# Seven products in the first feed-forward stage, moved modulation sections, and the mixers' two-operand work on VectorE

## The chip, the core and the metric

The kernel runs on one core of a Trainium2 chip. The metric is device time in microseconds (us). TensorE (PE) multiplies and PEld loads its weights, VectorE (DVE), ScalarE (ACT) and GpSimd (POOL) do the elementwise work, SyncE (SP) issues the transfers. A 32-bit value is multiplied as a high and a low part (both in the matmul's 32-bit format), and one product takes three matmuls: high by high, high by low, low by high.

## The reference

640 tokens (128 of a prompt, 512 of a grid) of width 1024 go through two layers. Each layer has three sublayers: a feed-forward network of width 2816, a mixer of three head groups, and a second feed-forward network. A modulation made from the condition scales, shifts and gates each of them.

```python
def swiglu(u, lp, j):
    return (jax.nn.silu(u @ lp['ffn_w_gate'][j]) * (u @ lp['ffn_w_up'][j])) @ lp['ffn_w_down'][j]
...
def trunk_layer(x, cond, lp, ropes, ctx):
    mod = (jax.nn.silu(cond) @ lp['w_mod'] + lp['b_mod'])[:, None, :]
    sh1, sc1, g1, sh2, sc2, g2, sh3, sc3, g3 = jnp.split(mod, N_MOD, axis=-1)
    x = layer_norm(DEEPNORM_ALPHA * x + 0.5 * g1 * swiglu(x * (1 + sc1) + sh1, lp, 0), lp['ln_g'][0], lp['ln_b'][0])
    y, ctx_out = mixer(x * (1 + sc2) + sh2, lp, ropes, ctx)
    x = layer_norm(DEEPNORM_ALPHA * x + g2 * y, lp['ln_g'][1], lp['ln_b'][1])
    x = layer_norm(DEEPNORM_ALPHA * x + 0.5 * g3 * swiglu(x * (1 + sc3) + sh3, lp, 1), lp['ln_g'][2], lp['ln_b'][2])
    return x, ctx_out
```

The mixer projects its input to 1696 columns, runs a recurrent scan, a grouped attention and a latent attention side by side, and projects back.

## The kernel before

**Stages.** The program is a list of steps in six stages: f00, m0, f01 (layer 0) and f10, m1, f11 (layer 1). f is a feed-forward network, m a mixer. The program text sets the order of TensorE's instructions. VectorE and ScalarE run in an order that a scheduler fixes at build time, in which `high_priority(offset=...)` moves an instruction ahead. All engines take their instructions in that fixed order. The weights come as 512 KB tiles through SP's queue into shared buffers (`raw`), in the order of the steps.

**A feed-forward stage.** The 2816 hidden columns are 22 m-tiles of 128. For each tile a gate and an up weight tile are split into a high part (L194, ScalarE) and a low part (L199, VectorE). In the classic form (`mtile`, L526 to L528) gate and up take 96 matmuls of 128x320 each tile. In the form with seven products (`ffn_fast`, L1083) the gate and up matrices of a tile are blocks of a 2x2 product that needs seven block products in place of eight, 84 matmuls; sums of the weight blocks (L1051), their splits (L1055 on ScalarE, L1059 on VectorE) and sums of the input are made for it, and the products are gathered by L1113 to L1137. f01, f10 and f11 use it from tile 3 on (`CLASSIC = 3`). f00 has a function of its own, `ffn_steps`, with the classic form for all 22 tiles. After every three tiles a down product (L821 to L823 in f00, L1195 to L1197 in the others) multiplies the hidden tiles with the down weights. f00 scales each down result by the gate (L828, VectorE) and adds it to the residual (L830, POOL). The others add the plain result to a sum (L1208, VectorE), having put x in DRAM, and scale and blend at the end.

**The opening of f00.** Modulation sections of layer 0 are needed before anything else. Tiles 0 and 1 are multiplied without the shift, which is added as a late bias (L674 and L679), and tile 2 follows (`start2`).

**Sections.** A section (layer, index) is one 1024-wide ninth of the modulation: eight 512 KB weight tiles, multiplied with two conditions. On TensorE it is eight steps, each of which the trace shows as 8 matmuls (L364). On VectorE it is 32 instructions of 128x512 (L329, L331), and 16 short matmuls (L340) sum over the partitions at the end. `PLAN` says in which stage a section stands. Those in a mixer's list and the one in `start2` run on TensorE, those in the third list of a feed-forward stage on VectorE. In `ffn_fast` they are fed by `trickle`, one instruction for every `MGAP` turns of the step list.

**A mixer.** Projections of 128 columns (`proj`, split by L194 and L199), the scans (L1386 to L1467), the norms and rotary products (L1523 to L1545), the attention (L1888 scores, L1902 and L1903 row maxima, L1904 exponentials, L1913 scaling on POOL, L1922 and L1850), and the output projection, whose result is scaled (L2279) and added to the residual (L2282). `ONV` names the two-operand instructions that `eng` puts on VectorE; the others are POOL's.

Of the kernel before, what the change touches and what calls it, by code (L numbers as in the profile page):

```python
# [18 lines left out]
P = 128  # L19
# [37 lines left out]
ONV = ('ladd', 'lix', 'mqg', 'swk0')  # L57
# [26 lines left out]
MGAP = 12  # L84
# [25 lines left out]
class Kern:  # L110
# [456 lines left out]
    def ffn_steps(self, l, j, mods):  # L567

        nc, I = self.nc, self.I
        env = {}  # L570
        S = []

        def B(dt=F32):
            return env["pool"].tile([P, TOK], dt, tag="B", bufs=11, name=self.nm("b"))

        def DW(shape):
            return env["pool"].tile(shape, F32R, tag="DW", bufs=8, name=self.nm("dw"))

        def T(shape):
            return env["pool"].tile(shape, F32, tag="T", bufs=3, name=self.nm("t"))  # L580

        def G4(shape):
            return env["pool"].tile(shape, F32, tag="G", bufs=4, name=self.nm("g"))

        jj = (0, 2)[j]
        hs = {}
        halves = {}
        dws = []
        for m in range(NM):
            g, u, d = {}, {}, {}  # L590
            fs = slice(m * P, (m + 1) * P)
            halves[m] = (g, u, d)

            def w_in_view(w):
                return w[l, j][:, fs].rearrange("(k p) f -> p k f", p=P)
# [3 lines left out]
            dl, dsp = self.weight(I["ffn_w_down"][l, j][fs, :], [P, D], d, DW)  # L599

            def silu(g, cut=HALF):
                for a, b in self.chunks(g["s"], g["ps"], cut):
                    nc.scalar.activation(a, b, AF.Silu)

            def hout(m, g, u, cut=HALF):
                s = g["s"]
                for a, b in self.chunks(s, u["ps"], cut):
                    nc.vector.tensor_mul(a, a, b)
                hh, hl = B(F32R), B(F32R)
# [4 lines left out]
            dws.append((dl, dsp))  # L614
            late_g, late_d = ((), ()) if m == 0 else LATE[l == 0 and j == 0].get(m, ((), (m,)))

            def gbody(m=m, g=g, late=[fn for i in late_g for fn in dws[i][1]]):
                g["ps"] = self.p2("pg")
                g["s"] = B()
                late = list(late)  # L620
                for c in range(2):
                    for _ in self.mtile(g["ps"], g, c):
                        yield
                        for _ in range(min(2, len(late))):
                            late.pop(0)()
                for fn in late:
                    fn()
                silu(g)


            def ubody(m=m, g=g, u=u, late=[fn for i in late_d for fn in dws[i][1]]):
                u["ps"] = self.p2("pu")
                if l == 0 and j == 0 and m == 4:
                    for i in range(DEPTH):
                        self.setup_vec(i)
                late = list(late)
                for c in range(2):
                    for _ in self.mtile(u["ps"], u, c):
                        yield
                        if late:  # L640
                            late.pop(0)()
                for fn in late:
                    fn()
                hout(m, g, u)

            def first(m=m, g=g, u=u):
                env["cm"] = self.tc.tile_pool(name=f"ffn{l}{j}", bufs=1, reuse_waits="tile")
                env["pool"] = env["cm"].__enter__()
                self.B_DW = DW
                g["ps"], u["ps"] = self.p2("pu"), self.p2()  # L650
                g["s"] = B()
                yield from self.mtile(g["ps"], g, 0, CUT)
                self.after_a()
                yield from self.mtile(u["ps"], u, 0, CUT)
                yield from self.mtile(g["ps"], g, 1, CUT)
                silu(g, CUT)
                yield from self.mtile(u["ps"], u, 1, CUT)
                hout(m, g, u, CUT)

            def biased(m, g, u):  # L660
# [29 lines left out]
                hh, hl = B(F32R), B(F32R)  # L690
                nc.scalar.copy(hh, s)
                nc.vector.tensor_sub(hl, s, f(hh))
                hs[m] = (hh, hl)
# [7 lines left out]
            def start(gsp, usp, g1=g, u1=u):  # L701


                g0, u0, _ = halves[0]
# [24 lines left out]
                env["cm"] = self.tc.tile_pool(name=f"ffn{l}{j}", bufs=1, reuse_waits="tile")  # L729
# [23 lines left out]
            def start2(m=m, g=g, u=u):  # L753

                g["ps"], u["ps"] = self.p2(), self.p2()
                g["s"] = B()
                todo = deque(self.next_steps)
                for h, k0 in ((g, 0), (u, 0), (g, 4), (u, 4)):
                    if k0 and self.late_bias:
                        self.bg.append(self.late_bias.pop(0)())  # L760
                    for k in range(k0, k0 + 4):
                        self.block(h, k)
                        yield CAP2 if h is u and k >= 6 else 0
                        if not todo:
                            continue
                        st = todo.popleft()
                        while not st.ready():
                            self.feed()
                        for _ in st.body():
                            yield  # L770
                silu(g)
                hout(m, g, u)
                if OEND == 2:
                    self.order.__exit__(None, None, None)
            if l == 0 and j == 0 and m == 0:
                self.first_w = gl, gsp, ul, usp
                S.append(None)
            elif l == 0 and j == 0 and m == 1:
                ul, usp = self.weight(w_in_view(I["ffn_w_up"]), [P, KT, P], u, lambda s: self.X(s, F32R))
                S[0] = Step([lambda i=i: self.shift_load(i) for i in range(4, 8)], [], lambda a=gsp, b=usp, go=start: go(a, b))  # L780
                self.second_w = gl, ul
                S.append(Step())
                S.append(Step())
            elif l == 0 and j == 0 and m == 2:
# [4 lines left out]
                lds = [gl, ul] + [st.loads[0] for st in self.next_steps] + [dws[i][0] for i in late_d]  # L789
                S.append(Step(lds, gsp + usp, start2, 0))  # L790
                S.append(Step([], [fn for i in late_d for fn in dws[i][1]]))
            elif m == 0:
                S.append(Step([gl, ul], gsp + usp, first))
            elif l == 0 and j == 0 and m == 3:
                S[-2].loads.insert(G3, gl)
                S.append(Step([dws[i][0] for i in late_g], gsp, gbody))
                S.append(Step([ul] + [dws[i][0] for i in late_d], usp, ubody))
            else:
                S.append(Step([gl] + [dws[i][0] for i in late_g], gsp, gbody))
                S.append(Step([ul] + [dws[i][0] for i in late_d], usp, ubody))  # L800
            S.extend(mods.get(m, []))


        def down(ci, ms):
            def body():
                lastc = ci == len(CHUNKS) - 1
                if ci == 0:
                    env["gate"] = self.gate_tiles(l, jj, G4, True)
                if lastc:
                    self.ln_begin(l, jj)  # L810
                for t in range(NT):
                    gt = env["gate"][1 if t == 0 else 0]
                    x = self.x[t]
                    for h in range(2):
                        pt = self.p1()
                        for i, m in enumerate(ms):
                            hh, hl = hs[m]
                            d = halves[m][2]
                            hsl = slice(h * 512, (h + 1) * 512)
                            ts = slice(t * P, (t + 1) * P)  # L820
                            nc.tensor.matmul(pt, lhsT=hh[:, ts], rhs=d["hi"][:, hsl], start=(i == 0), stop=False)  # L821
                            nc.tensor.matmul(pt, lhsT=hh[:, ts], rhs=d["lo"][:, hsl], start=False, stop=False)
                            nc.tensor.matmul(  # L823
                                pt, lhsT=hl[:, ts], rhs=d["hi"][:, hsl], start=False, stop=(i == len(ms) - 1)
                            )
# [5 lines left out]
                        if lastc:  # L831
                            self.ln_part(t, h, 2)
# [1761 lines left out]
```

## Time and profile before

| | before |
|---|---|
| median of 3 runs | 2546.53 us (2545.23 to 2547.19) |
| profiled execution | 2543.89 us, span 2541.8 us |
| PE busy | 2443.6 us (96%) |
| DVE, ACT, POOL busy | 74%, 42%, 16% |

The profiled execution has 2.1 us outside its span. TensorE's matmul records overlap, since each is shown from its start to a modelled end; what a matmul costs in a row of them is the distance from one start to the next.

### The profile page before, as it was taken

To read this page: it belongs to the slowest core of one execution; us is meant where nothing else is said; L and a number is where in the kernel's file an instruction comes from. 1 tells how busy PE (TensorE), PEld (TensorE's weight loads), DVE (VectorE), ACT (ScalarE), POOL (GpSimd) and SP (SyncE) were. 2 spreads that over 40 slices of the span, in tenths; PEclk is the share of its full clock that TensorE was granted. 3 is DMA by queue.
4 is the path that set the end of the run, shared out by engine and by line. 5 is a ranking of instruction groups with operands and counts; after the bars stand their busy time and mean duration, and the time that the engine had idled before them with its cause. 6 is when DMAs were issued, how large, how long until landed. Compare 5 with 4: busy or idle time off the path is not lost. (4 is left out here: it accounts for less than half of the span.)

```text
span 2541.8 us, 39941 instructions
## 1 busy us (share of the span) xinstructions
PE 2443.6 (96%) x15804; PEld 2218.4 (87%) x15804; DVE 1891.1 (74%) x3161; ACT 1068.9 (42%) x1882; POOL 411.2 (16%) x389
## 2 busy tenths in 40 slices
PE   8899999999999999999999999999999999999997
PEld 7789898988867999999889999988987799999986
DVE  5887778687754797777789777778785578777777
ACT  3212111246674444343354434435657534433432
POOL 2320221113632100000200000020373210000022
PEclk9999999999999999999999999999999999999999
DMA  8655445522233233333333333332232323333321
GB/s 286 197 152 155 141 147 185 158 69 80 95 90 113 67 132 111 98 100 100 108 91 124 113 96 100 100 108 82 91 112 90 97 76 100 110 107 104 113 92 50
DMA packets 271394, 288.53 MB, mean 114 GB/s; under 512 B 13436, under 2 KB 223976, under 8 KB 271208
## 3 DMA queue, kind: packets, MB, share of 16 engines
q1 hardware_dynamic: 271208, 285.99, 36.3%
q8 instruction: 124, 2.03, 0.3%
q14 instruction: 62, 0.51, 0.1%
HBM read 268.17 MB, written 16.21 MB: 112 GB/s over the span
## 5 line engine op out<-in xcount | busy, mean ns | idle before, releaser
L1083 PE MATMUL pb<-u,w 128*128 128x320 f32 x2736 | 420.4, 309 | 1.7 <-DVE b L1129 1.7
L1083 PEld LDWEIGHTS pb<-u,w 128*128 128x128 f32 x2736 | 406.7, 188 | 4.0 <-issue 2.4
L526 PE MATMUL p<-u,w 128*128 128x320 f32 (+2 forms) x1104 | 348.3, 316 | 8.6 <-ACT u L517 6.4
L527 PE MATMUL p<-u,w 128*128 128x320 f32 (+2 forms) x1104 | 345.8, 314 | 1.8 <-DVE u L518 1.8
L528 PE MATMUL p<-u,w 128*128 128x320 f32 (+2 forms) x1104 | 344.4, 313 | 0.0
L1083 PE MATMUL pb<-s,w 128*128 128x320 f32 x2052 | 322.0, 309 | 1.3 <-ACT b L1136 1.3
L1083 PEld LDWEIGHTS pb<-s,w 128*128 128x128 f32 x2052 | 306.0, 188 | 3.7 <-ACT b L1136 1.9
L1055 ACT CAST w<-raw 128x512 fp32r<-128x512 f32 x399 | 239.8, 619 | 162.8 <-DVE raw L1051 107.5
L1059 DVE TENSOR_TENSOR w<-raw,w 128x512 fp32r<-128x512 f32 x399 | 272.6, 696 | 34.9 <-ACT w L1055 34.2
L194 ACT CAST dw<-raw 128x1024 fp32r<-128x1024 f32 x87 | 89.1, 1051 | 452.6 <-PE p L1196 263.9
L331 DVE SCALAR_TENSOR_TENSOR x<-raw,cst,x 128x512 f32<-128x512 f32 x308 | 236.9, 815 | 33.3 <-DMA raw<-in_w_mod 33.2
L1195 PE MATMUL p<-dw,b 128*128 128x512 f32 x630 | 249.7, 396 | 11.3 <-DVE x L1208 10.1
L1196 PE MATMUL p<-dw,b 128*128 128x512 f32 x630 | 245.8, 390 | 0.0
L1197 PE MATMUL p<-dw,b 128*128 128x512 f32 x630 | 245.5, 390 | 0.0
L526 PEld LDWEIGHTS p<-u,w 128*128 128x128 f32 x1104 | 211.5, 192 | 13.7 <-ACT u L517 7.4
L527 PEld LDWEIGHTS p<-u,w 128*128 128x128 f32 x1104 | 211.7, 192 | 2.9 <-DVE u L518 2.5
L528 PEld LDWEIGHTS p<-u,w 128*128 128x128 f32 x1104 | 211.1, 192 | 0.3 <-DVE w L199 0.3
L194 ACT CAST w<-raw 128x1024 fp32r<-128x1024 f32 x100 | 104.8, 1050 | 241.3 <-PE p L527 162.3
L1208 DVE TENSOR_TENSOR x<-x,p 128x512 f32<-128x512 f32 x150 | 102.8, 685 | 110.5 <-PE p L1197 110.5
L1195 PEld LDWEIGHTS p<-dw,b 128*128 128x128 f32 x630 | 118.2, 188 | 47.3 <-DVE x L1208 21.6
L199 DVE TENSOR_TENSOR w<-raw,w 128x1024 fp32r<-128x1024 f32 x100 | 124.1, 1242 | 44.6 <-ACT w L194 40.5
L1157 POOL TENSOR_SCALAR x<-x 128x1024 f32<-128x1024 f32 x6 | 6.3, 1056 | 871.1 <-PE p L1197 438.3
(367 smaller groups left out, 4815.7 us busy)
## 6 DMA issues: line engine op xcount, KB each, us to landing
raw<-in_w_mod SPq DMA_DIRECT2D x132, 512.0 KB
raw<-in_ffn_w_gate SPq DMA_DIRECT2D x88, 512.0 KB
raw<-in_ffn_w_up SPq DMA_DIRECT2D x88, 512.0 KB
raw<-in_ffn_w_down SPq DMA_DIRECT2D x88, 512.0 KB
raw<-in_w_in SPq DMA_DIRECT2D x26, 512.0 KB
xd<-x SPq DMA_DIRECT2D x25, 512.0 KB
raw<-in_w_out SPq DMA_DIRECT2D x16, 512.0 KB
t<-xd SPq DMA_DIRECT2D x30, 256.0 KB
```

The lines of the kernel that those rows point to most:

```text
L194: nc.scalar.copy(h, hold["raw"])
L199: nc.vector.tensor_sub(l, hold["raw"], f(hold["hi"]))
L331: e.scalar_tensor_tensor(acc[:, cs], hold["raw"][:, cs], c, acc[:, cs], op0=ALU.mult, op1=ALU.add)
L526: nc.tensor.matmul(out, lhsT=wh, rhs=xh, start=start, stop=False)
L527: nc.tensor.matmul(out, lhsT=wh, rhs=xl, start=False, stop=False)
L528: nc.tensor.matmul(out, lhsT=wl, rhs=xh, start=False, stop=stop)
L1055: nc.scalar.copy(w[:, 0], at(src))
L1059: nc.vector.tensor_sub(w[:, 1], at(src), f(w[:, 0]))
L1083: nc.tensor.matmul(out, lhsT=a1, rhs=b1, start=(start and k == 0 and i == 0), stop=(k == 3 and i == 2), skip_group_check=not start,)
L1195: nc.tensor.matmul(pt, lhsT=hh[:, ts], rhs=d["hi"][:, cs], start=(i == 0), stop=False)
L1196: nc.tensor.matmul(pt, lhsT=hh[:, ts], rhs=d["lo"][:, cs], start=False, stop=False)
L1197: nc.tensor.matmul(pt, lhsT=hl[:, ts], rhs=d["hi"][:, cs], start=False, stop=(i == len(ms) - 1))
```

## The change

`ffn_steps` goes. Layer 0's first feed-forward stage is made by `ffn_fast` too: `opening` has tiles 0 to 2 (the late bias for 0 and 1, tile 2 in `third`), tile 3 is classic, and tiles 4 to 21 take seven products. The stage therefore writes x to DRAM and blends at its end as the others do; the first down product has tiles 0 to 2. Section (0,2) leaves TensorE for VectorE. VectorE's sections go from 8, 1, 1, 1 in f00, f01, f10, f11 to 3, 2, 2, 1; TensorE's from one in f00 and two in each mixer to five in m0 and three in m1. The gap of `trickle` follows the number of sections in the stage: 11 turns for one, 5 for two, 3 for three. In the mixers the splits of the projection weights are issued with priority, and seven two-operand instructions (named in `ONV`, the rotary product of the latent query, the addition to the residual) move from POOL to VectorE.

```diff
-ONV = ('ladd', 'lix', 'mqg', 'swk0')
+ONV = ('ladd', 'lix', 'lir', 'lmul', 'mqg', 'mkg', 'swk0', 'swk1', 'swq0', 'swq1')
...
-    "f00": [[], [], [(0, 3), (0, 4), (0, 5), (0, 6), (0, 7), (1, 0), (1, 1), (1, 2)]],
-    "m0": [[], [(0, 8), (1, 3)]],
-    "f01": [[], [], [(1, 4)]],
-    "f10": [[], [], [(1, 5)]],
-    "m1": [[], [(1, 6), (1, 7)]],
+    "f00": [[], [], [(0, 2), (0, 3), (0, 4)]],
+    "m0": [[], [(0, 5), (0, 6), (0, 7), (0, 8), (1, 0)]],
+    "f01": [[], [], [(1, 1), (1, 2)]],
+    "f10": [[], [], [(1, 3), (1, 4)]],
+    "m1": [[], [(1, 5), (1, 6), (1, 7)]],
...
-MGAP = 12
+MGAP = 12, 11, 5, 3
...
+                parts(m, g["s"], lambda: self.X([P, TOK], F32R))
+                self.order.__exit__(None, None, None)
+                self.x_d = [self.dp.tile([P, D], F32, name=self.nm("xd")) for _ in range(NT)]
+                for t in range(NT):
+                    nc.sync.dma_start(out=self.x_d[t], in_=self.x[t])
...
+        opens = l == 0 and j == 0
+        classic = CLASSIC + opens
...
+        if opens:
+            S += self.opening(env, hs, B, DW)
+            gate, up = plain(3)
+            for m in range(3):
+                dl, dsp = down_w(m)
+                gate.loads.append(dl)
+                S.append(Step([], dsp))
+            S[-3:] = [gate] + S[-3:] + [down([0, 1, 2], begin=True), up]
...
+        gap = MGAP[sum(len(v) for v in mods.values()) // KT]
...
-                        for _ in range(MGAP):
+                        for _ in range(gap):
...
-                nc.gpsimd.tensor_mul(
+                nc.vector.tensor_mul(
...
+        def urgent(fns):
+
+
+            def wrap(fn):
+                def go():
+                    with self.tc.high_priority(offset=AHEAD):
+                        fn()
...
+            sp = urgent(sp)
...
-                        e = nc.vector if last else nc.gpsimd
-                        e.tensor_add(x[:, cs], x[:, cs], tt)
+                        nc.vector.tensor_add(x[:, cs], x[:, cs], tt)
...
-            plan = spread(PLAN[f"f{l}0"], *((4,) if l == 0 else (4, 16)))
-            new = self.ffn_steps(l, 0, plan) if l == 0 else self.ffn_fast(l, 0, plan)
+            plan = spread(PLAN[f"f{l}0"], *((5, 17) if l == 0 else (4, 16)))
+            new = self.ffn_fast(l, 0, plan)
```

The order of three places shows what moved. First, TensorE in the opening of f00, the end of tile 2's first half (L526 to L528 the tile's matmuls, L364 a step of section (0,2), L666 the late bias). Before:

```order
L526 MATMUL p_80_714<-u_130,dw_680 128x320
L527 MATMUL p_80_714<-u_132,dw_680 128x320
L528 MATMUL p_80_714<-u_130,dw_686 128x320
L364 MATMUL p_82_722<-raw_729,cst 32x256 x4
L526 MATMUL p_79_713<-u_131,dw_640 128x320
L527 MATMUL p_79_713<-u_133,dw_640 128x320
L528 MATMUL p_79_713<-u_131,dw_652 128x320
```

Of the change:

```order
L526 MATMUL p_80_714<-u_130,dw_680 128x320
L527 MATMUL p_80_714<-u_132,dw_680 128x320
L528 MATMUL p_80_714<-u_130,dw_686 128x320
L526 MATMUL p_79_713<-u_131,dw_640 128x320
L527 MATMUL p_79_713<-u_133,dw_640 128x320
L528 MATMUL p_79_713<-u_131,dw_652 128x320
```

The last of the section's eight steps stood there; none of them is left in this tile.

Second, VectorE in f00. Before, at a down product (L828 scales it) and the tile that follows (L608 multiplies gate and up, L611 and L199 split, L331 and L329 are section instructions):

```order
L331 SCALAR_TENSOR_TENSOR x_2621<-raw_2619,cst,x_2621 128x512 x2
L828 TENSOR_TENSOR t_2414<-p_306_2401,g_1054 128x512
L828 TENSOR_TENSOR t_2430<-p_308_2417,g_1057 128x512
L828 TENSOR_TENSOR t_2446<-p_310_2433,g_1054 128x512
L828 TENSOR_TENSOR t_2462<-p_312_2449,g_1057 128x512
L828 TENSOR_TENSOR t_2478<-p_314_2465,g_1054 128x512
L828 TENSOR_TENSOR t_2494<-p_316_2481,g_1057 128x512
L828 TENSOR_TENSOR t_2510<-p_318_2497,g_1054 128x512
L199 TENSOR_TENSOR dw_2562<-raw_2253,dw_2544 128x1024
L199 TENSOR_TENSOR dw_2721<-raw_2342,dw_2703 128x1024
L828 TENSOR_TENSOR t_2526<-p_320_2513,g_1057 128x512
L608 TENSOR_TENSOR b_2313<-b_2313,p_322_2529 128x640
```

Of the change, at a tile of seven products in the same stage (L898 differences of weight blocks, L906 their splits, L960 to L984 gather the products, L760 splits the hidden tile, L331 as before):

```order
L331 SCALAR_TENSOR_TENSOR x_2026<-raw_1917,cst,x_2026 128x512
L331 SCALAR_TENSOR_TENSOR x_2025<-raw_2070,cst,x_2025 128x512 x2
L960 TENSOR_TENSOR pb_1241<-pb_1241,b_2047 128x320
L331 SCALAR_TENSOR_TENSOR x_2026<-raw_2070,cst,x_2026 128x512
L962 TENSOR_TENSOR pb_1239<-pb_1239,b_2047 128x320
L976 TENSOR_TENSOR b_1882<-pb_1240,b_1882 128x320
L906 TENSOR_TENSOR w_2119<-raw_2093,w_2119 128x512
L331 SCALAR_TENSOR_TENSOR x_2026<-raw_2070,cst,x_2026 128x512
L898 TENSOR_TENSOR raw_2093<-raw_2109,raw_2093 128x512
L331 SCALAR_TENSOR_TENSOR x_2025<-raw_2082,cst,x_2025 128x512 x2
L979 TENSOR_TENSOR b_2132<-b_2132,pb_1238 128x320
L906 TENSOR_TENSOR w_2142<-raw_2093,w_2142 128x512
```

Section instructions now stand between the instructions on which the next product waits.

Third, VectorE in the first mixer, among the scans (before: L1440 and L1455, of the change L1303, L1304 and L1318; L199 is the low half of a projection's weight split, L1304 the product that was POOL's L1441). Before:

```order
L1440 SCALAR_TENSOR_TENSOR b_5471<-b_5625,b_5471 128x644
L1440 SCALAR_TENSOR_TENSOR b_5517<-b_5641,b_5517 128x644
L1440 SCALAR_TENSOR_TENSOR b_5563<-b_5658,b_5563 128x644
L1455 SCALAR_TENSOR_TENSOR b_5821<-b_5625,b_5493 128x128
L1455 SCALAR_TENSOR_TENSOR b_5821<-b_5625,vec_108,b_5493 128x512
L199 TENSOR_TENSOR w_5799<-raw_4993,w_5774 128x1024
```

Of the change:

```order
L1318 SCALAR_TENSOR_TENSOR b_5654<-b_5455,vec_108,b_5298 128x512
L1303 SCALAR_TENSOR_TENSOR b_5322<-b_5476,b_5322 128x644
L1304 TENSOR_TENSOR b_5344<-b_5344,b_5322 128x644
L199 TENSOR_TENSOR w_5650<-raw_4464,w_5625 128x1024
L1303 SCALAR_TENSOR_TENSOR b_5368<-b_5492,b_5368 128x644
L199 TENSOR_TENSOR w_5688<-raw_4483,w_5670 128x1024
```

The splits stand before the third scan step of four instead of behind the second scan, and L1304 is new on VectorE.

## Rows read from the trace of the kernel before

**Rows 1.** The page, busy time: us, share of the span, instructions.

```profile
PE 2443.6 (96%) x15804; PEld 2218.4 (87%) x15804; DVE 1891.1 (74%) x3161; ACT 1068.9 (42%) x1882; POOL 411.2 (16%) x389
```

**Rows 2.** Windows: stretch, length, busy us by engine, granted clock, DMA share, GB/s.

```profile
0.00:545.00 545.00, 519.09 (x3411) 468.38 (x3411) 405.75 (x586) 138.28 (x187) 105.30 (x91) 0.99 0.54 168
545.00:875.00 330.00, 313.44 (x2349) 275.90 (x2350) 220.67 (x436) 192.91 (x353) 116.41 (x117) 0.97 0.29 92
875.00:1320.00 445.00, 436.94 (x2596) 403.97 (x2595) 347.92 (x572) 187.14 (x343) 19.74 (x17) 1.00 0.34 102
...
16.00:96.00 80.00, 74.27 (x697) 66.20 (x690) 54.04 (x78) 33.61 (x51) 21.71 (x17) 0.96 0.86 281
...
916.00:1280.00 364.00, 360.12 (x2150) 334.20 (x2150) 276.96 (x448) 148.28 (x274) 16.27 (x12) 1.00 0.37 111
...
655.00:805.00 150.00, 142.88 (x1067) 107.49 (x1066) 89.40 (x216) 105.41 (x205) 57.45 (x66) 1.00 0.33 105
```

**Rows 3.** TensorE's waits, whole span: total us, times, longest.

```profile
PE p L821 <- DVE t L828: 10.3, 15, 1.3
PE p L527 <- DVE w L199: 10.2, 6, 3.0
PE p L1195 <- DVE x L1208: 10.1, 27, 0.8
...
PE p L679 <- DVE b L674: 4.5, 1, 4.5
```

**Rows 4.** Timeline of TensorE: start, length, instruction; f00, then f01.

```profile
122.67 0.31 PE L526 MATMUL p<-u,w 128*128 128x320 f32 x1
122.81 0.31 PE L527 MATMUL p<-u,w 128*128 128x320 f32 x1
...
954.82 2.95 PE L1083 MATMUL pb<-s,w 128*128 128x320 f32 x19
```

**Rows 5.** Timeline of TensorE in f00: section matmuls between a tile's own.

```profile
58.40 0.64 PE L364 MATMUL p<-raw,cst 128*32 128x256 f32 x8
...
60.04 0.64 PE L364 MATMUL p<-raw,cst 128*32 128x256 f32 x8
...
157.90 0.31 PE L528 MATMUL p<-u,w 128*128 128x320 f32 x1
158.14 1.07 PE L340 MATMUL p<-x,sel 128*32 128x256 f32 x16
...
159.39 0.31 PE L527 MATMUL p<-u,w 128*128 128x320 f32 x1
```

**Rows 6.** Timeline of all engines in the opening, with idle before and releaser.

```profile
84.88 1.28 DVE L329 TENSOR_SCALAR x<-raw,cst 128x512 f32<-128x512 f32 x3 [4.90 <-DMA raw<-in_w_mod]
...
86.53 0.37 PE L679 MATMUL p<-ident,b 4*128 4x4 f32 x2 [4.45 <-DVE b L674]
```

**Rows 7.** VectorE's groups, 96 to 545 us, then 916 to 1280 us.

```profile
L331 DVE SCALAR_TENSOR_TENSOR x<-raw,cst,x 128x512 f32<-128x512 f32 x221 | 173.8, 842 | 25.4 <-DMA raw<-in_w_mod 25.4
...
L331 DVE SCALAR_TENSOR_TENSOR x<-raw,cst,x 128x512 f32<-128x512 f32 x28 | 20.3, 747 | 3.1 <-DMA raw<-in_w_mod 3.1
```

**Rows 8.** Windows of VectorE alone, products of f01 and f10.

```profile
960.00:980.00 20.00, 19.88 (x36) 1.00 0.34 100
...
1400.00:1420.00 20.00, 19.82 (x34) 1.00 0.52 153
```

**Rows 9.** Timeline of the first mixer, VectorE, then TensorE.

```profile
620.72 1.19 DVE L199 TENSOR_TENSOR w<-raw,w 128x1024 fp32r<-128x1024 f32 x1
...
621.96 0.39 PE L527 MATMUL p<-w,u 128*128 128x256 f32 x1 [2.96 <-DVE w L199]
```

**Rows 10.** Timeline of TensorE in the first mixer's attention.

```profile
671.48 2.35 PE L364 MATMUL p<-raw,cst 128*32 128x256 f32 x34 [0.58 <-ACT u L1761]
```

**Rows 11.** Groups of POOL and VectorE, whole span.

```profile
L2282 POOL TENSOR_TENSOR x<-x,b 128x256 f32<-128x256 f32 x20 | 18.3, 916 | 54.4 <-DVE b L2279 50.2 <-DMA raw<-in_ffn_w_down 4.1
...
L2282 DVE TENSOR_TENSOR x<-x,b 128x256 f32<-128x256 f32 x20 | 8.4, 422 | 0.4
```

More of the change, by code (lines that the diff above doesn't have):

```diff
@@ L564, in chunks, with opening, parts @@
         return [(s[:, 0:cut], pt[:, 0, 0:cut]), (s[:, cut:TOK], pt[:, 1, 0 : TOK - cut])]
-    def ffn_steps(self, l, j, mods):
+    def opening(self, env, hs, B, DW):
         nc, I = self.nc, self.I
-        env = {}
         S = []
[L573 to L586, printed above, removed]
         halves = {}
-        dws = []
-        for m in range(NM):
-            g, u, d = {}, {}, {}
+        for m in range(3):
+            g, u = {}, {}
             fs = slice(m * P, (m + 1) * P)
-            halves[m] = (g, u, d)
+            halves[m] = (g, u)
             def w_in_view(w):
-                return w[l, j][:, fs].rearrange("(k p) f -> p k f", p=P)
+                return w[0, 0][:, fs].rearrange("(k p) f -> p k f", p=P)
             gl, gsp = self.weight(w_in_view(I["ffn_w_gate"]), [P, KT, P], g, self.W)
             ul, usp = self.weight(w_in_view(I["ffn_w_up"]), [P, KT, P], u, self.W)
[L599 to L609, printed above, removed]
+            def parts(m, s, alloc):
+                hh, hl = alloc(), alloc()
                 nc.scalar.copy(hh, s)
@@ L612, in hout @@
                 hs[m] = (hh, hl)
[L614 to L658, printed above, removed]
             def biased(m, g, u):
@@ L689, in biased @@
                     )
[L690 to L693, printed above, removed]
+                parts(m, s, lambda: B(F32R))
             def kept(g, u):
@@ L788, in ffn_steps @@
                     fn.ready = lambda h=h: "DW" in env and "raw" in h
[L789 to L825, printed above, removed]
-                        tt = T([P, 512])
-                        with self.tc.high_priority(offset=AHEAD):
-                            nc.vector.tensor_mul(tt, pt, gt[h])
-                        e = nc.vector if lastc and (FA or h or t == NT - 1 or self.next_mod) else nc.gpsimd
-                        e.tensor_add(x[:, hsl], x[:, hsl], tt)
-                        if lastc:
-                            self.ln_part(t, h, 2)
-                        yield
-                    if lastc:
-                        self.end_tile(t)
-                if lastc:
-                    env["cm"].__exit__(None, None, None)
-            return Step([], [], body)
@@ L869, in ffn_steps @@
-        out.append(down(*pend))
-        return out
+                S.append(Step([gl, ul], gsp + usp, third, 0))
+        return S
     def ffn_fast(self, l, j, mods):
@@ L952, in gate @@
             def gate():
+                if opens:
+                    env["sums"] = sums()
+                    self.bg.append(env["sums"])
                 g["ps"] = self.p2()
@@ L1174, in body @@
                 if begin:
-                    for _ in self.res:
+                    for _ in () if opens else self.res:
                         pass
@@ L1229, in ffn_fast @@
             S += st + mods.get(m, [])
-        dl, dsp = down_w(CLASSIC - 1)
+        dl, dsp = down_w(classic - 1)
         S[-1].loads.append(dl)
@@ L1262, in rest, with vecs @@
             yield
-        seq = [("A", CLASSIC), ("A", CLASSIC + 1), ("D", 2)]
-        for m in range(CLASSIC, NM):
+        def vecs():
+            for i in range(DEPTH):
+                self.setup_vec(i)
+            yield
+        seq = [("A", classic), ("A", classic + 1)] + ([] if opens else [("D", 2)])
+        for m in range(classic, NM):
             seq.append(("B", m))
@@ L1275, in ffn_fast @@
                 S += part_a(m)
+                if opens and m == classic:
+                    S.append(Step([], [], vecs))
             elif what == "B":
@@ L2030, in mixer_steps @@
         S = []
+        def urgent(fns):
[3 more added lines that the diff above has]
+                        fn()
+                go.ready = fn.ready
+                return go
+            return [wrap(fn) for fn in fns]
         def proj(c0, post, first=None):
```

68 lines of the change are left out of this document (16 added, 52 removed).

## Prediction

> **What bounds the kernel now.** I read the busy table first [rows 1]: TensorE is busy for 96% of the span, VectorE for 74%, no other engine for half. The time is therefore TensorE's work plus its waits. The windows by stage come next [rows 2]: f00 takes 545 us, f01 445 us, the first mixer 330 us. The reader is to see that f00 and f01 do the same network, and that f00 is 100 us longer. Part of that is the start, part the 12 more matmuls of each of its m-tiles, part its sections. Then TensorE's waits [rows 3]: none is large. f00's down products wait 10.3 us for the scaled result (15 times), f01, f10 and f11 together 10.1 us for the added one (27 times), the mixers' projections 10.2 us for a weight split, the late bias 4.5 us once. So work that is taken from TensorE counts nearly in full, as long as VectorE keeps up. That is the second thing to read: in f01 VectorE is busy for 276.96 of 364 us [rows 2], 76%, but in stretches of pure products for 19.88 and 19.82 of 20 us [rows 8]. It runs full there already and catches up in the down products.
>
> **Seven products in f00.** A busy row overstates a matmul, since records overlap. In f00 one of 128x320 starts 0.14 us after the other, and in f01 19 in a row take 2.95 us, of which the last one's own 0.31 is to be taken off: 2.64/18 = 0.147 us [rows 4]. Tiles 4 to 21 lose 96 - 84 = 12 matmuls each: 18 x 12 = 216, by 0.147 = **-31.8 us**. This is the term that nothing hides.
>
> **Section (0,2) off TensorE.** From one step of it to the next 1.64 us pass, with six of the tile's matmuls between [rows 5]: 1.64 - 6 x 0.147 = 0.76 us a step, eight steps, **-6.1 us**. A VectorE section still costs TensorE its 16 summing matmuls: from 157.90 to 159.39 us with two ordinary matmuls, 1.49 - 0.29 = 1.2 us [rows 5]. f00 has five fewer, **-6.0**; f01 and f10 have one more each, **+2.4**.
>
> **Waits in f00.** The 10.3 us go with the instructions that wait. The other stages' form waits 10.1/3 = 3.4 us a stage [rows 3]: **-6.9**. In the opening the late bias waits 4.45 us for a small copy on VectorE that stands behind a section's first instruction, which itself waited 4.90 us for its weights [rows 6]. In the changed order the sections start only after tile 4, so nothing late is ahead of that copy: **-4.5**. What is late next there are the input sums for the seven products and the low parts of tiles 0 to 2, all on VectorE; I put that into the next term. The opening also issues five 512 KB writes of x, and three down tiles earlier than before. It drops eight section tiles that were loaded there, and the queue reached 281 GB/s between 16 and 96 us against 168 over the stage [rows 2]. I cost the transfers at nothing, for the range at up to 5 us.
>
> **VectorE in f00.** The stage's 96 section instructions all stand between tiles 4 and 14 of the changed order. f01's window holds 2150 matmuls in 364 us, and a tile has 84 and a third of the 90 of a down product, 114: 18.9 tiles, 19.3 us each [rows 2]. Eleven tiles are 212 us of TensorE. VectorE's other work is that of f01: 276.96 less the section's 20.3 is 256.7 in 364 us, a share of 0.705 [rows 2, 7], so 149 us of these 212. The sections add 96 x 0.842 = 81 us (0.747 in f01, rows as far apart as this stage is [rows 7]). Together 230 us against 212: VectorE is short by 18 us, and TensorE has to wait for it. From tile 15 on VectorE has room, but lateness is not given back. The bounds: 5 us if the shortness is partly taken by buffers and the cheaper 0.747 holds (221 against 212, half of it hidden), 35 if the queue's order adds waits at each insertion. The row that it is nearest to is the product stretch at 99% busy that cost nothing, so I take the plain difference and 2 us for the opening's sums, **+20**.
>
> f00 in all: -31.8 - 6.1 - 6.0 - 6.9 - 4.5 + 20 = -35.
>
> **f01 and f10.** 32 more section instructions in each, 27 us by 0.842: f01's VectorE goes from 347.92 to 375 of 445 us [rows 2], 84%. TensorE's work covers that; without that cover it would be up to 10 us in each. I take 0 beside the 2.4 us above.
>
> **The mixers.** m0 gets three more sections on TensorE, m1 one. A step costs 0.76 us in a row of products [rows 5], in a burst of 34 matmuls 2.35 us [rows 10], that is 64 x 2.35/34 = 4.4 us a section. They stand in the attention, where TensorE's records fill 142.88 of 150 us [rows 2] but overlap, and short chains through ScalarE, VectorE and POOL leave holes between bursts. Bounds: 0 if all four fall into holes, 4 x 6.1 = 24 if none does. I take half, **+12**. Their 32 loads more (24 in m0, 12.6 MB over 150 us, +84 GB/s on 105) stay under 281 GB/s [rows 2]. Against this stand the 10.2 us that projections wait for their low weight half; the longest is 2.96 us, with the split behind the scans on VectorE [rows 3, 9]. Priority moves the splits some places forward, not to the front: 0 to 10, I take **-6**. The additions to the residual take 916 ns on POOL and 422 on VectorE [rows 11], and all that moves takes VectorE some 11 us in a stage where it is busy for 220.67 of 330 [rows 2]; shorter chains at the norms and at the end: 0 to 10, I take **-4**. The mixers together: +2.
>
> **The sum.** -35 + 2.4 + 2 = -31. The profiled execution took 2543.9 us (span 2541.8, 2.1 around it), 2.6 under the median shown. 2543.9 - 31 = 2513; I forecast **2513 us**, own range 2502 to 2526.
>
> **Rivals.**
>
> *VectorE keeps up.* The insertions fall into the slack of the down products (f01's product stretches at 99% lost TensorE nothing), and the shortness is 3 in place of 20; the mixers' gains come in full (-20 + 12). Then -52 + 2.4 - 8 = -58, **2486 us**. For it: no wait over 1.3 us in f00's down products [rows 3] although VectorE took 221 section instructions there [rows 7]. Against it: that was the classic form, which has none of the weight sums.
>
> *The mixers take it back.* TensorE sections in the attention are not hidden (+24), the splits still stand behind the scans (0), f01 and f10 lose 5 each: -35 + 2.4 + 24 + 10 = +1 at the worst, half way to it -15, **2529 us**. For it: section bursts that follow ScalarE's release directly [rows 10]. Against it: the attention's engines all have room.
>
> *VectorE's queue becomes the bound (slower).* Section instructions stand between the splits and the gathers on which the next product waits. One whose weights are late holds everything behind it, as in the opening, 4.90 us on VectorE and 4.45 on TensorE [rows 6]. f00 loads 24 such weight tiles between its tiles 4 and 14; twelve waits of this size in f00 are 53 us, and f01 and f10 at 10 each add 20. Then -55 + 20 + 53 + 20 + 2.4 + 2 = +42 at the worst; at half of the added waits +6, **2550 us**. It decides from about 31 us of waits beyond my 20, seven like that of the opening. Against it: section weights waited only 25.4 us on VectorE over the whole of f00 at 221 instructions [rows 7], and mostly without TensorE.
> [...]
>
> **Chances.** Forecast 0.48, VectorE keeps up 0.24, the mixers take it back 0.17, the queue as bound 0.11. The range holds 8 in 10 if it goes from the middle of the second case to just short of the last: 2486 to 2543. A difference of 0.2% (5 us) is what a measurement of this kernel can tell from none. Faster by more than that: the first two, most of the third, 0.86; within it 0.07; slower 0.07.
>
> **What would show it.** f00 should end near 510 us after the start in place of 545, with no L526 to L528 after tile 3. If the product term is right, a seven-product tile there takes 84 matmuls 0.147 us apart. If the VectorE term is right, TensorE's waits between tiles 4 and 14 add up to about 20 us, on the weight splits (L906) and gathers (L960 to L984), and VectorE is at 95% or more there; after tile 14 the waits stop. If VectorE keeps up, those waits are under 5 us. f01 and f10 should be as long as before within 4 us. In m0 the attention should be some 9 us longer and the projections' waits shorter. The prediction is wrong if f00 ends after 530 us, or if the mixers differ by more than 12 us from before.

## The result and the profile after

The changed kernel took 2524.6 us (2520.8 to 2526.3, 4 runs) beside 2545.9 us before (2544.6 to 2547.2, 4 runs): a ratio of 0.9914, 95% interval 0.9897 to 0.9931. It is 21 us faster, in the forecast's direction and inside its range (by 1.4 us inside the narrow one, 2502 to 2526), but two thirds of the 31 us that it stated. Measured a second time it was 2519.5 against 2539.9 us, 0.9921 (0.9906 to 0.9936). The runs below were made on three chips, each beside the kernel before, so ratios and not times are compared.

The profiled execution has a span of 2524.0 us. The page's busy times, which answer to [rows 1]:

```profile
PE 2422.2 (96%) x15732; PEld 2189.8 (87%) x15732; DVE 1945.6 (77%) x3389; ACT 1135.7 (45%) x2062; POOL 290.9 (12%) x291
```

The windows by stage, with the columns of [rows 2]; each stage ends at the last transposes of its norm (L506):

```profile
0.00:501.90 501.90, 476.53 (x3043) 434.00 (x3044) 405.15 (x673) 207.11 (x370) 44.29 (x49) 0.99 0.46 142
501.90:839.50 337.60, 323.19 (x2545) 277.24 (x2543) 229.55 (x475) 191.41 (x350) 87.28 (x89) 0.99 0.39 128
839.50:1289.50 450.00, 439.12 (x2614) 404.36 (x2613) 367.54 (x605) 186.22 (x342) 20.19 (x17) 1.00 0.36 111
1289.50:1740.70 451.20, 438.69 (x2610) 404.37 (x2609) 369.49 (x617) 189.66 (x348) 21.73 (x22) 0.99 0.37 114
1740.70:2074.90 334.20, 316.94 (x2408) 275.74 (x2407) 227.09 (x471) 190.58 (x350) 86.18 (x89) 0.98 0.32 102
2074.90:2524.00 449.10, 427.77 (x2525) 394.09 (x2523) 346.74 (x554) 170.73 (x307) 31.23 (x25) 0.98 0.32 98
```

Read the same way, by the last L506 of each norm, the stages of before are 543.8, 330.7, 445.2, 444.9, 326.0 and 451.2 us. So f00 gave 41.9 us, and four of the other five took back 26.2: m0 6.9, f01 4.8, f10 6.3, m1 8.2. f11 gave 2.1. In all -17.8, the difference of the spans. The reader is to see that the gain is where the edit is large, and that the loss is spread over stages in which less was edited.

TensorE's waits, which answer to [rows 3]:

```profile
PE p L1042 <- DVE x L1055: 15.7, 35, 1.4
...
PE p L527 <- DVE w L199: 5.0, 4, 1.6
PE p L595 <- DVE shr L2329: 4.9, 1, 4.9
```

The down products (L1042 here, L1195 before) now wait 15.7 us in four stages, where the two forms together waited 20.4. The projections' wait for a weight split fell from 10.2 to 5.0 us. The opening's wait did not go: 4.5 us in [rows 3, 6], 4.9 now, at another place. The timeline of the opening, VectorE, then TensorE:

```profile
62.51 7.69 DVE L2320 SCALAR_TENSOR_TENSOR b<-u,sh,u 128x128 f32<-128x128 f32 x8
71.10 1.50 DVE L2329 TENSOR_TENSOR shr<-sh,shr 128x16 fp32r<-128x16 f32 x1 [0.90 <-ACT shr L2328]
...
72.65 3.58 PE L595 MATMUL p<-w,shr 128*4 128x128 f32 x32 [4.85 <-DVE shr L2329]
```

The late bias needs the two halves of the shift (`shr`), and these come at the end of a chain. The shift itself is there at 50.1 us; its halves are made by L2328 on ScalarE and L2329 on VectorE, which stand behind the shifting of the input (L2320 and L2321), though they need nothing of it. Of VectorE, then ScalarE:

```profile
49.95 0.17 DVE L2301 TENSOR_TENSOR sh<-p,bcol 128x8 f32<-128x8 f32 x1 [0.57 <-PE p L2300]
...
70.23 0.72 ACT L2321 CAST u<-b 128x640 fp32r<-128x640 f32 x1 [2.79 <-DVE b L2320]
70.86 0.20 ACT L2328 CAST shr<-sh 128x16 fp32r<-128x16 f32 x1
```

Before, the halves came behind the same chain, and TensorE did not wait:

```profile
67.70 1.52 DVE L2453 TENSOR_TENSOR shr<-sh,shr 128x16 fp32r<-128x16 f32 x1 [0.90 <-ACT shr L2452]
...
71.43 2.08 PE L666 MATMUL p<-w,shr 128*4 128x128 f32 x32
```

Counted from the first step of that chain, TensorE is at the late bias 5.9 us earlier than before, mostly since the section's eight steps no longer stand in tile 2, and the halves come 1.1 us later, since one more weight split (L199) stands ahead of them. The wait is 4.84 or 4.85 us in all twelve runs that have this opening.

Between 110 and 322 us, tiles 4 to 14 of f00, the window of VectorE alone (busy, clock, DMA share, GB/s) and its two largest groups:

```profile
110.00:322.00 212.00, 195.20 (x323) 1.00 0.45 137
```

```profile
L331 DVE SCALAR_TENSOR_TENSOR x<-raw,cst,x 128x512 f32<-128x512 f32 x78 | 56.8, 743 | 3.3 <-DMA raw<-in_w_mod 3.2
L906 DVE TENSOR_TENSOR w<-raw,w 128x512 fp32r<-128x512 f32 x77 | 51.7, 684 | 6.7 <-ACT w L902 6.5
```

VectorE is 92% busy, and TensorE waits for almost nothing (waits, same stretch):

```profile
PE pb L930 <- DVE w L906: 0.9, 2, 0.5
PE pb L930 <- ACT w L902: 0.8, 2, 0.7
```

The prediction looked for about 20 us here. Gaps that overlapping records hide are not in these 1.7 us: from start to start, the 894 matmuls of the seven products in this stretch take 0.1504 us each on average, 3 us more in all than at their median of 0.147.

### The profile page after: what moved, and what is told of

Its sections match the earlier page's. It is cut to its first block, busy times and chain, and to the rows that moved or that the text cites. A ratio compares the mean times of both kernels' runs of the same rounds, so it can differ in the third digit from the quotient of the medians.

```text
span 2524.0 us, 40100 instructions
## 1 busy us (share of the span) xinstructions
PE 2422.2 (96%) x15732; PEld 2189.8 (87%) x15732; DVE 1945.6 (77%) x3389; ACT 1135.7 (45%) x2062; POOL 290.9 (12%) x291
## 5 line engine op out<-in xcount | busy, mean ns | idle before, releaser
L930 PE MATMUL pb<-u,w 128*128 128x320 f32 x3600 | 554.5, 309 | 2.2 <-DVE b L976 2.2
L930 PEld LDWEIGHTS pb<-u,w 128*128 128x128 f32 x3600 | 534.8, 188 | 6.8 <-issue 4.3
L930 PE MATMUL pb<-s,w 128*128 128x320 f32 x2700 | 424.7, 310 | 3.9 <-ACT b L983 2.1
L902 ACT CAST w<-raw 128x512 fp32r<-128x512 f32 x525 | 316.0, 619 | 229.9 <-DVE raw L898 148.4
L930 PEld LDWEIGHTS pb<-s,w 128*128 128x128 f32 x2700 | 402.4, 188 | 9.2 <-ACT b L983 3.1
L906 DVE TENSOR_TENSOR w<-raw,w 128x512 fp32r<-128x512 f32 x525 | 356.2, 690 | 44.6 <-ACT w L902 43.5
L1042 PE MATMUL p<-dw,b 128*128 128x512 f32 x830 | 329.6, 397 | 17.4 <-DVE x L1055 15.7
L1043 PE MATMUL p<-dw,b 128*128 128x512 f32 x830 | 323.9, 390 | 0.0
L1044 PE MATMUL p<-dw,b 128*128 128x512 f32 x830 | 323.6, 390 | 0.0
L1042 PEld LDWEIGHTS p<-dw,b 128*128 128x128 f32 x830 | 155.7, 188 | 66.6 <-DVE x L1055 32.8
L1044 PEld LDWEIGHTS p<-dw,b 128*128 128x128 f32 x830 | 155.8, 188 | 33.1
L1043 PEld LDWEIGHTS p<-dw,b 128*128 128x128 f32 x830 | 155.9, 188 | 29.2
L331 DVE SCALAR_TENSOR_TENSOR x<-raw,cst,x 128x512 f32<-128x512 f32 x224 | 163.5, 751 | 20.4 <-DMA raw<-in_w_mod 20.4
L526 PE MATMUL p<-u,w 128*128 128x320 f32 (+2 forms) x528 | 167.6, 319 | 7.1 <-ACT u L517 6.8
L527 PE MATMUL p<-u,w 128*128 128x320 f32 (+2 forms) x528 | 166.7, 317 | 1.3 <-DVE u L518 1.3
L528 PE MATMUL p<-u,w 128*128 128x320 f32 (+2 forms) x528 | 165.3, 315 | 0.0
L199 DVE TENSOR_TENSOR dw<-raw,dw 128x1024 fp32r<-128x1024 f32 x86 | 105.3, 1228 | 43.7 <-ACT dw L194 43.7
L898 DVE TENSOR_TENSOR raw<-raw,raw 128x512 f32<-128x512 f32 x150 | 103.0, 687 | 10.1 <-DMA raw<-in_ffn_w_up 8.2
```

Of the source, the lines that this page charges most:

```text
L199: nc.vector.tensor_sub(l, hold["raw"], f(hold["hi"]))
L331: e.scalar_tensor_tensor(acc[:, cs], hold["raw"][:, cs], c, acc[:, cs], op0=ALU.mult, op1=ALU.add)
L526: nc.tensor.matmul(out, lhsT=wh, rhs=xh, start=start, stop=False)
L527: nc.tensor.matmul(out, lhsT=wh, rhs=xl, start=False, stop=False)
L528: nc.tensor.matmul(out, lhsT=wl, rhs=xh, start=False, stop=stop)
L902: nc.scalar.copy(w[:, 0], at(src))
```

## The experiments

All stage lengths are of one profiled execution each, read as above; the ratios are of repeated runs to the kernel before on the same chip. "Sections" are those of f00, m0, f01, f10, m1, f11; in the mixers they run on TensorE, as does one of the nine in f00 before.

| kernel | sections | ratio (95%) | f00 | m0 | f01 | f10 | m1 | f11 |
|---|---|---|---|---|---|---|---|---|
| before | 9, 2, 1, 1, 2, 1 | 1 | 543.8 | 330.7 | 445.2 | 444.9 | 326.0 | 451.2 |
| changed | 3, 5, 2, 2, 3, 1 | 0.9914 (0.9897 to 0.9931) | 501.9 | 337.6 | 450.0 | 451.2 | 334.2 | 449.1 |
| after_again (the changed kernel once more) | the same | 0.9921 (0.9906 to 0.9936) | 502.1 | 339.8 | 448.5 | 450.3 | 330.1 | 448.1 |
| mixers_only | 9, 2, 1, 1, 2, 1 | 1.0020 (1.0010 to 1.0029) | 543.9 | 331.0 | 446.2 | 444.1 | 326.2 | 450.0 |
| engines_back | 3, 5, 2, 2, 3, 1 | 0.9896 (0.9881 to 0.9911) | 502.4 | 337.9 | 449.3 | 449.5 | 328.5 | 448.0 |
| no_urgent | the same | 0.9894 (0.9878 to 0.9911) | 502.3 | 337.3 | 449.6 | 449.8 | 331.1 | 449.1 |
| ffn_only | the same | 0.9917 (0.9902 to 0.9932) | 501.9 | 338.3 | 446.8 | 447.3 | 336.1 | 449.4 |
| sections_out | 4, 2, 3, 4, 2, 1 | 0.9970 (0.9960 to 0.9979) | 519.1 | 327.5 | 449.6 | 461.3 | 329.2 | 450.3 |
| deal_mixers | 3, 7, 1, 1, 3, 1 | 0.9889 (0.9874 to 0.9904) | 501.9 | 342.0 | 445.9 | 444.9 | 329.4 | 446.0 |
| deal_ffn | 3, 3, 3, 3, 3, 1 | 0.9886 (0.9870 to 0.9903) | 501.5 | 331.3 | 447.9 | 449.4 | 333.6 | 447.3 |
| deal_full | 3, 3, 3, 3, 3, 1 | 0.9900 (0.9886 to 0.9915) | 500.4 | 332.5 | 449.0 | 450.3 | 335.5 | 449.0 |
| deal_m1 | 3, 4, 3, 3, 2, 1 | 0.9878 (0.9863 to 0.9893) | 500.7 | 335.6 | 448.5 | 448.3 | 327.6 | 447.5 |
| f00_gap2 | 3, 5, 2, 2, 3, 1 | 0.9909 (0.9895 to 0.9924) | 499.5 | 338.5 | 449.3 | 449.8 | 331.5 | 449.6 |
| light_sections | the same | 0.9908 (0.9892 to 0.9925) | 497.6 | 339.1 | 448.4 | 449.2 | 331.7 | 449.2 |

**What the mixers' part does alone.** On the kernel before:

```diff
-ONV = ('ladd', 'lix', 'mqg', 'swk0')
+ONV = ('ladd', 'lix', 'lir', 'lmul', 'mqg', 'mkg', 'swk0', 'swk1', 'swq0', 'swq1')
...
+            sp = urgent(sp)
...
-                        e = nc.vector if last else nc.gpsimd
-                        e.tensor_add(x[:, cs], x[:, cs], tt)
+                        nc.vector.tensor_add(x[:, cs], x[:, cs], tt)
```

> The kernel before, with the mixers' part of the change alone: priority for the projection splits, and the two-operand work on VectorE. Sections and f00 as before. Theory 1 (a section on TensorE in a mixer costs its whole 5 to 6 us, the rest of the mixers' part gains): m0 about 8 us shorter than before (330.7 to 322), m1 2 to 5 us shorter (326.0 to 322), the rest unchanged, 2534 to 2537 us against 2546. Theory 2 (the attention became longer because VectorE now has the two-operand work, and the sections are hidden): both mixers about 8 us longer, 2560 us or more.

Both theories missed. The mixers are as long as before, 331.0 and 326.2 us, and the kernel is 0.2% slower rather than faster. (The profiled execution was the fastest of ten, so its stages do not show where the 0.2% lie.) The first score maximum comes 4.0 us earlier after the start of m0 (107.2 in place of 111.2), since the projections' waits shrink (L527 on L199 from 5.5 to 2.4 us in m0). But of the 48 maxima the second is 3.7 us early, the third 1.7, the sixth 1.1 late, and from the seventh to the last all are 0.4 to 0.5 late. The gain is gone within 27 us. TensorE's timeline there:

```profile
664.66 0.66 PE L2012 MATMUL p<-ident,b 128*128 128x128 f32 x4 [1.54 <-POOL b L2007]
...
669.90 3.23 PE L364 MATMUL p<-raw,cst 128*32 128x256 f32 x56 [0.58 <-ACT u L1761]
...
674.91 0.62 PE L364 MATMUL p<-raw,cst 128*32 128x256 f32 x2 [1.08 <-DMA raw<-in_w_mod]
```

56 section matmuls stand in one burst where there were 34 [rows 10], a scaling on POOL is waited for, and then the section's weights are. It looks as if work that was hidden in later holes has moved ahead, and the rest of the attention comes at its old time; no run takes these apart.

**The sections out of the mixers.** In the changed kernel, with a gap of 2 for four sections:

```diff
-MGAP = 12, 11, 5, 3
+MGAP = 12, 11, 5, 3, 2
...
-    "f00": [[], [], [(0, 2), (0, 3), (0, 4)]],
-    "m0": [[], [(0, 5), (0, 6), (0, 7), (0, 8), (1, 0)]],
+    "f00": [[], [], [(0, 2), (0, 3), (0, 4), (0, 5)]],
+    "m0": [[], [(0, 6), (0, 7)]],
...
```

> The changed kernel, with the sections dealt out as 4, 2, 3, 4, 2, 1 to f00, m0, f01, f10, m1, f11 in place of 3, 5, 2, 2, 3, 1 (gap of 2 turns for four). Theory 1: m0 loses three sections on TensorE, 337.6 to about 322 us, m1 one, 334.2 to 328; f00 gets one more on VectorE, 501.9 to 503 if VectorE has room, to 510 if it has none; f01 and f10 get one and two, +2 to +4 and +3 to +10. In all 2508 to 2518 us against 2524. Theory 2: the mixers stay at 338 and 334, and the kernel is slower by what f01 and f10 pay, 2528 to 2536.

The mixers did what theory 1 said in kind, 327.5 and 329.2 us. But f00 took 17.2 us more for its fourth section, f10 10.1 more for its third and fourth (a third alone costs it nothing in the dealings below), and the kernel lost most of its gain. Between 110 and 322 us VectorE is no busier than with three sections, yet fewer tiles are done. Its window, and two of its groups:

```profile
110.00:322.00 212.00, 190.37 (x316) 1.00 0.46 137
```

```profile
L331 DVE SCALAR_TENSOR_TENSOR x<-raw,cst,x 128x512 f32<-128x512 f32 x89 | 64.0, 748 | 0.0
L906 DVE TENSOR_TENSOR w<-raw,w 128x512 fp32r<-128x512 f32 x67 | 44.2, 684 | 7.8 <-ACT w L902 7.8
```

11 section instructions more have taken the place of 10 weight splits. And the high parts on ScalarE (L902) wait longer for the gate weights' transfers, 32.2 us here. These share their buffers with the section tiles; in the changed kernel SP's queue waits 71.4 us in this stretch (50.1, 13.9 and 7.4, by the line that loads) for section instructions (L331). The waits of L902 here:

```profile
ACT w L902 <- DVE raw L898: 34.6, 13, 5.9
ACT w L902 <- DMA raw<-in_ffn_w_gate: 32.2, 9, 8.8
```

In the changed kernel its wait for the transfers is 14.0:

```profile
ACT w L902 <- DMA raw<-in_ffn_w_gate: 14.0, 6, 4.4
```

The prediction's third rival comes near this, one section further on: section instructions stand between the splits and the gathers. But its late section weights are not seen, since L331 waits 0.0 us. From start to start the 17.2 us are 9.0 in the seven products, 4.9 in the down products and 5.4 in the summing matmuls (L340), with some 2 us less in other matmuls.

**Is it the gap or the amount?**

```diff
-MGAP = 12, 11, 5, 3
+MGAP = 12, 11, 5, 2
```

> The changed kernel with a gap of 2 turns in f00 in place of 3, so that the three sections' instructions stand closer. With four sections at this gap f00 took 519 us. If the order at gap 2 did that, f00 goes from 502 to 510 us or more; if VectorE's capacity did (four sections of work in the room of three), f00 stays at 501 to 505.

f00 took 499.5 us: the closer order costs nothing. The fourth section's amount did it. Whether it is VectorE's time or the late gate weights is not told apart by these runs.

**What the section work on VectorE costs.**

```diff
+LIGHT = (0, 2), (0, 3), (0, 4), (1, 1), (1, 2), (1, 3), (1, 4)
...
+                        if k and (g or h) and (l, s) in LIGHT:
+                            continue
                         e = nc.gpsimd if (g, h) in VP else nc.vector
```

> The changed kernel with most of the sections' work in f00, f01 and f10 left out: of the 32 VectorE instructions of a section 21 are not issued, so these seven sections are not computed fully; their loads and their summing matmuls stay. It measures what their VectorE work costs. By the prediction's term (VectorE short by some 18 us between tiles 4 and 14 of f00) f00 falls from 502 to about 485 us; by its rival (VectorE keeps up) f00 stays within 4 us of 502, and f01 and f10, at 450, fall by less than 3 us each.

f00 fell by 4.3 us, f01 by 1.6, f10 by 2.0. Beside deal_full and deal_m1 below, which have the same sections in f00 and ran on the same chip, f00 fell by 2.8 and 3.1, and the kernel as a whole is no faster than f00_gap2, 0.9908 and 0.9909. So two thirds of the section instructions in f00 cost 3 to 4 us, not the 18 by which the prediction had VectorE short. VectorE's window:

```profile
110.00:322.00 212.00, 163.98 (x269) 1.00 0.47 144
```

54 instructions fewer, 31.2 us less busy. That is not the price of one, since VectorE got further with its other work in this window. The price stands in a row of them in the changed kernel:

```profile
131.64 2.07 DVE L331 SCALAR_TENSOR_TENSOR x<-raw,cst,x 128x512 f32<-128x512 f32 x3
```

Three take 2.07 us, where a record shows 0.743: the next one starts 0.663 us after the one before.

**The mixers' part taken out of the changed kernel**, by halves and whole:

```diff
-ONV = ('ladd', 'lix', 'lir', 'lmul', 'mqg', 'mkg', 'swk0', 'swk1', 'swq0', 'swq1')
+ONV = ('ladd', 'lix', 'mqg', 'swk0')
...
-            sp = urgent(sp)
```

> The changed kernel with the mixers' two-operand work on GpSimd again, as before the change; priority of the splits, sections and f00 as in the change. Theory 1: the mixers are longer than in the change by 2 to 5 us each, 2529 to 2534 us against 2524. Theory 2: they are shorter by 6 to 8 us each, 2508 to 2512.

> The changed kernel without the priority of the projection splits. Theory 1: TensorE's waits for a low weight half come back to about 5 us a mixer from 2.5, and each mixer is 2 to 4 us longer, 2528 to 2532 us. Theory 2 speaks of the engines alone and says the same or nothing, 2524 to 2532.

> The changed kernel once more, beside the next three. Theory 3 (the mixers' engine moves and priorities cost, in this kernel, 5 to 7 us): 2523 to 2527 us again, with the second mixer near 334 us. Rival (the earlier 6 us were the spread of runs): 2517 to 2521, second mixer near 329.

> The change without its mixers' part: two-operand work on GpSimd and no priority for the projection splits, as before the change; f00 by seven products and the sections as in the change. Theory 3: 2516 to 2520 us, the second mixer at 328 to 331. Rival: the same as the changed kernel in the same call within 3 us.

engines_back and no_urgent fit neither theory: each came out 5 to 6 us shorter than the changed kernel, as if each half cost that much, so theory 3 was formed. It fell: beside one another on one chip, the changed kernel and the one without its mixers' part have 0.9921 and 0.9917, and m0 takes 337 to 340 us in all five. In this kernel engines and priority are worth nothing that can be measured, in either direction. The front is shorter here too, and again nothing comes of it: the first score maximum comes 103.2 us after the start of m0 in the changed kernel and 107.9 in no_urgent, the last 259.7 in both. The 5 to 6 us were spread, most of it in m1.

**Dealing the sections anew**, on the kernel without the mixers' part (the first two) and on the changed one (the last two). For 3, 3, 3, 3, 3, 1 the edit is this, and the others follow the same pattern:

```diff
-    "m0": [[], [(0, 5), (0, 6), (0, 7), (0, 8), (1, 0)]],
-    "f01": [[], [], [(1, 1), (1, 2)]],
-    "f10": [[], [], [(1, 3), (1, 4)]],
+    "m0": [[], [(0, 5), (0, 6), (0, 7)]],
+    "f01": [[], [], [(0, 8), (1, 0), (1, 1)]],
+    "f10": [[], [], [(1, 2), (1, 3), (1, 4)]],
```

> The kernel without the mixers' part, with sections dealt 3, 7, 1, 1, 3, 1: one taken from f01 and one from f10, both to the first mixer, on TensorE. Theory 4 (a section more on VectorE costs f01 and f10 about 5 us each, one on TensorE in a mixer 2 to 3): f01 and f10 back to 445, m0 337.5 to 343, in all 4 to 6 us shorter than without the redealing. Rival (a section in a mixer costs its whole 5 to 6 us, and f01 and f10 became longer for another reason than the section): m0 348, f01 and f10 as they are, 10 us longer.

> The kernel without the mixers' part, with sections dealt 3, 3, 3, 3, 3, 1: two taken from the first mixer, one each to f01 and f10, on VectorE, with a gap of 3 turns. Theory 4: m0 337.5 to 333, f01 stays at 450 (it took 449.6 with three), f10 at 450 to 455, in all 0 to 5 us shorter. Rival: each costs f01 and f10 another 5 us and m0 gains 10: no change.

> The changed kernel with its mixers' part, sections dealt 3, 3, 3, 3, 3, 1. Without the mixers' part this dealing was 7 us shorter than without the redealing. If the mixers' part changes nothing, 0.988 to 0.990 of the kernel before; if it costs, 0.991 or more.

> The changed kernel, sections dealt 3, 4, 3, 3, 2, 1: one from the second mixer to the first. At 2.7 us a section on TensorE in either mixer it is the same as with 3, 3, 3, 3, 3, 1, within 2 us.

The first two came out near theory 4. m0 takes 331.3 us with three sections, 338.3 with five and 342.0 with seven: 2.7 us each, where the section that f00 had on TensorE took 4.6 from start to start. f01 and f10 take 444 to 446 with one, 447 to 451 with two, 448 to 450 with three, so only the second costs something. Both dealings are about 7 us shorter than ffn_only on the same chip (2511 against 2518 us). deal_full at 0.9900 is not told apart from deal_ffn by the intervals. deal_m1 was the best kernel of the study, 2510.7 against 2543.4 us, 0.9878: its interval lies below both of the changed kernel's, and overlaps those of deal_ffn, deal_mixers and deal_full. Its expectation missed: it is 6.5 us shorter than deal_full, not the same within 2, and the difference is in m1 (327.6 and 335.5 us). Its executions show a mean granted clock of 0.993 to 0.995, those of deal_full 0.990 to 0.991, so the dealing is not shown to have done it.

## Why the prediction was right in sign, and where its sum was off

**Products, -31.8: right.** f00's gate and up matmuls take 329.2 us before and 300.3 after, summed from start to start, with what they wait: -28.9. What VectorE makes them wait is in that.

**Section (0,2) off TensorE, -6.1, and the opening's wait, -4.5: the first somewhat large, the second failed.** The section's matmuls took 4.6 us from start to start and are gone. But they stood where TensorE would otherwise have waited for the halves of the shift, and the wait is 4.85 us now in place of 4.45. The step "nothing late is ahead of that copy" looked at what stands before the copy on VectorE, and not at the next link, the shift's own chain.

**Summing matmuls, -6.0 in f00: nearly right**, 8.0 us became 3.0. **Down products, -6.9: right**, 166.3 us became 159.4.

**VectorE in f00, +20: this term failed.** The section work costs 3 to 4 us (light_sections). Two errors made it. The first is the price of 0.842 us an instruction. In the kernel before it is the mean of 178 records of 0.746 us and of 43 that ran beside an addition to the residual on POOL (L830), 1.24 on average. One of these:

```profile
107.97 1.73 POOL L830 TENSOR_TENSOR x<-x,t 128x512 f32<-128x512 f32 x1 [1.23 <-DVE t L828]
108.47 1.78 DVE L331 SCALAR_TENSOR_TENSOR x<-raw,cst,x 128x512 f32<-128x512 f32 x1
```

The change itself takes these additions out of the tiles. POOL alone between 110 and 322 us, before, then after:

```profile
110.00:322.00 212.00, 41.82 (x26) 1.00 0.47 144
...
110.00:322.00 212.00, 1.30 (x1) 1.00 0.45 137
```

And a record was taken as cost, although the text had said of TensorE that records overlap; from start to start it is 0.663 us. At that, 84 of the 96 instructions and the 12 that begin a sum (L329, 0.396) take 60 us in place of 81, and 149 + 60 = 209 of 212 us is no shortage. The second error is the share of 0.705 for its other work, from a window of f01 that also holds work which does not recur in tiles 4 to 14 of f00 (L1169, L2347, L2348): there 195.20 less 56.5 for the 90 section instructions leaves 139 of 212, 0.65. So f00 gave 41.9 us, 7 more than the 35 forecast. The rival "VectorE keeps up" was right on this term, though not in its -52 for f00. The margin is thin all the same: one section more costs 17 us.

**f01 and f10, +2.4 together: too small.** They took 11.1. light_sections gives back 3.6 of it with two thirds of the section work left out, and only 1.5 beside f00_gap2 on the same chip. The down products' wait rises by 2 us in f01, before, then after:

```profile
PE p L1195 <- DVE x L1208: 3.3, 9, 0.4
...
PE p L1042 <- DVE x L1055: 5.4, 10, 1.3
```

The rest is not settled: ffn_only has the same sections, 3.2 us of that wait, and took 446.8 and 447.3.

**Mixers, +2: the cost was right, the gains failed.** Sections +12 for four; at 2.7 us each they measure 11. Against it stood -6 for priority and -4 for VectorE, and both together gained nothing (mixers_only 1.0020): the shortened front is lost again in the attention. The profile has +15; the 4 us that the sections don't explain are within what m1 varies by (below). The second rival, "the mixers take it back", was right that the gains do not come and that f01 and f10 lose 10; its +24 for sections that are not hidden was 11.

By stage, f00 gave 7 us more than forecast (some 17 less lost to VectorE, 10 less gained by the other terms) and f11 2, f01 and f10 took 9 more, the mixers 13: by the profiled spans -17.8 in place of -31. Errors of opposite sign met, and that the time lies in the narrow range is luck: the profiled execution, 2525.9 us, is 13 us from the forecast's 2513 and 3 from the second rival's 2529. By the prediction's own signs f00 came out as the first rival has it (it ended at 502 us, with 1.7 us of waits between tiles 4 and 14, under the 5 named), f01 and f10 moved by more than the 4 us allowed, and the mixers, 15.1 us longer together (13.2 in after_again), by more than the 12 that it named as a sign of being wrong.

The opening shows again what the third rival built on, ready work behind an instruction that waits: ScalarE idled 2.79 us before L2321 at 70.23, while the cast L2328 behind it had had its input since 50.1, and TensorE's 4.85 us followed. On VectorE all 3161 instructions in the trace of before, and all 3389 in that of the change, start in the order of the program, line by line. sections_out is a case in which section instructions stand ahead of what TensorE waits for; no run gives the number from which that costs.

## What to carry to other kernels

Records overlap on VectorE (0.743 us shown, 0.663 from start to start) as on TensorE (0.309 shown in a product, 0.147 from start to start): price an added instruction by the distance from one start to the next in a full row, not by its record, and look at what ran beside it where the price was read (0.746 us, or 1.24 beside an addition on POOL). When work is taken away from the engine that sets the time, look for what it covered, to the second link: here a wait of the same size stood right behind it, for two small instructions whose input had long been ready. A shorter front of a stage is worth nothing until the stage's end is seen to move: the 4.0 us at the front of m0 were gone within 27.

## What the runs showed that was not expected

m1 varies more than any other stage. In two executions of the changed kernel it took 334.2 and 330.1 us, and with one code and the same sections 336.1, 329.4 and 333.6 in ffn_only, deal_mixers and deal_ffn. The windows of that stage in the first two, ffn_only, then deal_mixers:

```profile
1734.30:2070.40 336.10, 320.98 (x2410) 280.12 (x2408) 221.87 (x446) 191.55 (x351) 114.71 (x117) 0.96 0.31 102
```

```profile
1734.70:2064.00 329.30, 312.10 (x2409) 271.44 (x2408) 221.92 (x447) 191.33 (x350) 115.67 (x117) 0.99 0.32 104
```

The mean granted clock is 0.96 in the one and 0.99 in the other. In the changed kernel's m1 the window from 1948 to 1957 us has a clock of 0.50, and that from 1960 to 2060 has 1.00; that ffn_only spent more of the stage at such a lower clock is an estimate from the means. deal_ffn had 0.99 as well, so the clock is not the whole of it. A few us in m1 of one profile are no verdict, which is how theory 3 came up and fell.
